# Expert weights in 4096-byte runs, shared rows written plainly, three experts in two passes, another order of experts

## The chip, the cores and the metric

The kernel runs on one core of a Trainium2 chip. The core has TensorE (PE) for matrix products with its own weight load (PEld), VectorE (DVE), ScalarE (ACT), GpSimd (POOL) and SyncE (SP), and 16 DMA engines that move data between HBM and the on-chip memory. Plain loads and stores are issued here by SP (queue q1 in the profile), gathers and scatter-adds by POOL (queue q0). The metric is the device time of one run in microseconds (us).

## The reference, cut to what matters

One decoder layer is computed for 1032 tokens (1024 of a prompt, 8 of decoding requests) of width 1024: a projection, two branches (RWKV-7 mixing and latent attention), a layer norm, and then a mixture of experts, which is what the change touches:

```python
def _swiglu(x, wg, wu, wd):
    return (jax.nn.silu(x @ wg) * (x @ wu)) @ wd

def _moe(h, P):
    ...
    _, e_idx = lax.top_k(jnp.where(e_mask, sb, -jnp.inf), TOP_K)        # 8 of 64 experts for a token
    ...
    routed = _routed_experts(h, e_idx, wts, P['w_exp_gate'], P['w_exp_up'], P['w_exp_down'])
    return routed + _swiglu(h, P['w_sh_gate'], P['w_sh_up'], P['w_sh_down'])
```

Each of the 64 experts has three fp32 matrices of 1024 x 256 elements (gate, up, down), 1 MB each, so 3 MB for an expert and 192 MB for all. Every token goes through 8 experts and through one shared expert of the same size. The results, weighted, are summed by token, and a last layer norm follows.

## The kernel before

The stages stand one behind the other: projections, the two branches, the output product with routing, the experts, the last norm. The experts take the last two fifths of the time.

**Ranks and capacities.** Experts are ranked on the chip by how many tokens chose them. For rank `r` the program is compiled for `CAPS[r]` rows: 480, 448, 416, 384, ... down to 68 for ranks 0 to 41, 64 for ranks 42 to 53, 32 for ranks 54 to 63. Only the expert's number is read at run time (`value_load` in `moe`, L2090), and it gives the address of the weights.

**Four ways to compute an expert.** From 200 rows up (`up_wide`) the gate and up weights are split in a high and a low part in fp32r (`part`: ACT writes `eph`, L1358, and DVE writes `epl`, L1361), the rows too, and three products are summed; the columns of a matrix product are the rows of the expert. From 65 to 128 rows (`up_rows`) the roles of weights and rows are exchanged. From 129 to 199 rows (`up_mid`) and up to 64 rows (`few`) the weights are used as they came, in plain fp32. The down product of all but `few` splits the down weights (`edh`, `edl`); what is left over at the end of an expert, up to 64 rows, goes through `down_rest` (L1967) with the plain weights.

**Loads.** SP issues them in the order of the program. `ffn_load` makes four tiles `egu` of 512 KB for an expert, each filled by two DMAs (gate and up, L1809), in which each partition reads 512 fp32 elements, a run of 2048 bytes; then two tiles `ewd` of 512 KB with the down weights (L1817), runs of 4096 bytes. There are 7 `egu` buffers (1.75 experts) and 6 `ewd` buffers (3 experts). A load waits until its buffer has been read by its last user, and whatever SP has behind it waits too. In `moe`, while expert `q` is computed, all of expert `q + 2` is issued.

**Rows.** For expert `q + 1` POOL gathers the rows of `h2D` with indirect DMAs of 128 KB (`xg`, L1841), DVE transposes them (L1844) into `xt` (two buffers, split into the one `xh`, `xl`) or, for `up_mid` and `few`, into `xf` (two buffers of 192 columns). Results are scaled by ACT and DVE into `ey` (four buffers of 1024 columns) and added to one of two accumulators in HBM, `accD`, by an indirect accumulating DMA from POOL (`add_rows`, L1981), taking turns.

**The shared expert** is computed first, in three passes of 360, 360 and 312 rows, with weights that are kept until the third pass has used them; its results are added to the accumulators like all others, by the index tile `IT`. Both accumulators are filled with zeros long before (20 DMAs of up to 512 KB, L1518).

**The order of the experts** is made by `order` (L2042): it takes large and row-exchanged experts in turn with middle and small ones, so that a running estimate of TensorE's lead over the loads stays near zero. By their rows the experts come as 128, 64, 120, 64, 112, 64, 112, 192, 108, 184, 480, 64, 104, 64, 448, 64, 100, 176, 96, 176, 416, 64, 92, 64, 384, ... and at the end 80, 136, 80, 32, 76, 32, 72, 32, 72, 32, 68, 32. The two later passes of the shared expert stand at places 0 and 1. Within this, a scheduler decides how the instructions of neighbouring experts are mixed on each engine.

## Time and profile before

| | us |
|---|---|
| median of 3 runs | 2481.7 (2474.22 to 2485.76) |
| the profiled execution | 2478.88 |
| its span, from the first to the last instruction | 2477.1 |
| start of routing's end and the shared expert | about 1385 |
| first routed expert computed from | about 1502 |
| last weights of an expert issued | 2377.9 |
| last norm's first loads of the sums | 2402.4 |

The page's own line on the span gives 86% for PE, 68% for PEld, 57% for DVE, 40% for ACT and 38% for POOL. These are averages over stages with different limits; the stage of the experts is read by itself, with windows. "DMA share" in such a window is the time that the packets took, divided by 16 engines times the window: it goes a little over 1 where packets overlap. The times of a window, a timeline row and a wait count from the start of the span.

### The profile page before, as it was taken

To read this page: it belongs to the slowest core of one execution; us is meant where nothing else is said; L and a number is where in the kernel's file an instruction comes from. 1 tells how busy PE (TensorE), PEld (TensorE's weight loads), DVE (VectorE), ACT (ScalarE), POOL (GpSimd) and SP (SyncE) were. 2 spreads that over 40 slices of the span, in tenths; PEclk is the share of its full clock that TensorE was granted. 3 is DMA by queue.
4 is the path that set the end of the run, shared out by engine and by line. 5 is a ranking of instruction groups with operands and counts; after the bars stand their busy time and mean duration, and the time that the engine had idled before them with its cause. 6 is when DMAs were issued, how large, how long until landed. Compare 5 with 4: busy or idle time off the path is not lost. (4 is left out here: it accounts for less than half of the span.)

```text
span 2477.1 us, 39847 instructions
## 1 busy us (share of the span) xinstructions
PE 2141.3 (86%) x14376; PEld 1695.0 (68%) x14376; DVE 1402.8 (57%) x2638; ACT 981.0 (40%) x1737; POOL 943.8 (38%) x799
## 2 busy tenths in 40 slices
PE   5999999978779998999689578899999998899754
PEld 3998999867557766578678466576767777677331
DVE  3544345511567865544657856566666666566437
ACT  3333332612445554222337434443443443344325
POOL 3243342021101001310216755467666566565226
PEclk8999999989789999999899699999999999899877
DMA  8146567454543424664999768999999999999994
GB/s 295 35 102 169 164 175 171 132 167 126 181 108 108 137 49 182 228 197 145 314 218 198 162 168 258 324 307 308 321 323 292 310 313 336 261 293 295 322 319 157
DMA packets 361507, 536.91 MB, mean 217 GB/s; under 512 B 118127, under 2 KB 219455, under 8 KB 354955
## 3 DMA queue, kind: packets, MB, share of 16 engines
q1 hardware_dynamic: 298330, 421.38, 53.3%
q0 software_dynamic: 60496, 112.63, 18.7%
q8 instruction: 114, 1.87, 0.3%
q10 hardware_dynamic: 2480, 0.33, 0.1%
q14 instruction: 87, 0.70, 0.1%
HBM read 410.97 MB, written 123.84 MB: 216 GB/s over the span
## 5 line engine op out<-in xcount | busy, mean ns | idle before, releaser
L1841 POOL DMA_INDIRECT xg<-h2D,IG x303 | 352.3, 1163 | 256.3 <-DVE xt L1844 92.2
L1361 DVE TENSOR_TENSOR epl<-egu,eph 128x1024 fp32r<-128x1024 f32 x140 | 169.5, 1217 | 114.6 <-ACT eph L1358 114.4
L147 PE MATMUL psup<-xh,eph 128*128 128x360 f32 (+15 forms) x576 | 184.8, 330 | 27.1 <-ACT xh L1358 19.2
L1358 ACT ACTIVATE eph<-egu 128x1024 fp32r<-128x1024 f32 x140 | 147.1, 1055 | 152.6 <-DMA egu<-in_w_exp_up_dram 87.7
L149 PE MATMUL psup<-xh,epl 128*128 128x360 f32 (+15 forms) x576 | 180.6, 326 | 10.7 <-DVE epl L1361 10.2
L148 PE MATMUL psup<-xl,eph 128*128 128x360 f32 (+15 forms) x576 | 186.0, 326 | 4.3 <-DVE xl L1361 4.2
L1981 POOL DMA_INDIRECT accD<-ey,IS x65 | 115.4, 1775 | 118.0 <-ACT ey L1974 57.6
L147 PE MATMUL psy<-edh,ehh 128*128 128x512 f32 (+12 forms) x296 | 127.1, 435 | 18.3 <-ACT ehh L1358 9.4
L1361 DVE TENSOR_TENSOR edl<-ewd,edh 128x1024 fp32r<-128x1024 f32 x90 | 108.5, 1217 | 54.6 <-ACT edh L1358 53.2
L147 PEld LDWEIGHTS psup<-xh,eph 128*128 128x128 f32 x576 | 113.3, 199 | 37.1 <-ACT xh L1358 21.3
L1358 ACT ACTIVATE edh<-ewd 128x1024 fp32r<-128x1024 f32 x90 | 94.0, 1053 | 89.2 <-PE psy L149 74.7
L147 PE MATMUL pwg<-hh,whg 128*128 128x344 f32 x384 | 126.7, 330 | 0.0
L149 PEld LDWEIGHTS psup<-xh,epl 128*128 128x128 f32 x576 | 111.6, 197 | 20.8 <-DVE epl L1361 11.9
L149 PE MATMUL pwg<-hh,wlg 128*128 128x344 f32 x384 | 125.2, 326 | 0.0
L148 PE MATMUL pwg<-hl,whg 128*128 128x344 f32 x384 | 125.0, 326 | 0.0
L148 PE MATMUL psy<-edl,ehh 128*128 128x512 f32 (+12 forms) x296 | 121.6, 416 | 0.0
L148 PEld LDWEIGHTS psup<-xl,eph 128*128 128x128 f32 x576 | 114.1, 198 | 10.4 <-DVE xl L1361 5.6
L1844 DVE STREAM_TRANSPOSE xt<-xg 128x1024 f32<-128x1024 f32 (+3 forms) x61 | 113.8, 1872 | 0.2
L149 PE MATMUL psy<-edh,ehl 128*128 128x512 f32 (+12 forms) x296 | 109.1, 412 | 0.6 <-DVE ehl L1361 0.5
L1994 PE MATMUL psup<-egu,xf 128*32 128x128 f32 (+1 forms) x1024 | 81.7, 335 | 23.9 <-DMA egu<-in_w_exp_up_dram 18.0
L1920 PE MATMUL psup<-xf,egu 128*128 128x176 f32 (+7 forms) x640 | 96.2, 304 | 1.9 <-DMA egu<-in_w_exp_gate_dram 1.8
L1920 PEld LDWEIGHTS psup<-xf,egu 128*128 128x128 f32 x640 | 92.1, 191 | 5.9 <-DMA egu<-in_w_exp_gate_dram 2.2
(723 smaller groups left out, 5747.8 us busy)
## 6 DMA issues: line engine op xcount, KB each, us to landing
egu<-in_w_exp_gate_dram SPq DMA_DIRECT2D x256, 256.0 KB
egu<-in_w_exp_up_dram SPq DMA_DIRECT2D x256, 256.0 KB
ewd<-in_w_exp_down_dram SPq DMA_DIRECT2D x128, 512.0 KB
wada<-in_w_ada_dram SPq DMA_DIRECT2D x24, 1024.0 KB
accD<-zero SPq DMA_DIRECT2D x18, 512.0 KB
gateD<-g SPq DMA_DIRECT2D x16, 516.0 KB
bg<-gateD SPq DMA_DIRECT2D x48, 172.0 KB
wrg<-in_w_in_dram SPq DMA_DIRECT2D x16, 512.0 KB
```

The lines of the kernel that those rows point to most:

```text
L147: nc.tensor.matmul(out, lh, rh, start=start, stop=False)
L148: nc.tensor.matmul(out, lh, rl, start=False, stop=False)
L149: nc.tensor.matmul(out, ll, rh, start=False, stop=stop)
L1358: nc.scalar.activation(hi, src, AF.Copy)
L1361: self.last_split = nc.vector.tensor_sub(lo, src, hi.bitcast(F32))
L1841: nc.gpsimd.indirect_dma_start(out=X[:, g, :], out_offset=None, in_=h4, in_offset=bass.IndirectOffsetOnAxis(ap=idx(j, g), axis=0))
L1844: nc.vector.transpose(out=dst.rearrange("p k (g b) -> p g k b", b=32), in_=X[:, 0:G, :].rearrange("p g (a k) -> p g k a", k=8))
L1920: nc.tensor.matmul(p[:, :C], gu[k // 2][:, j, k % 2, m * 128:(m + 1) * 128], xt[:, k, :C], start=(k == 0), stop=(k == 7))
L1981: self.nc.gpsimd.indirect_dma_start(out=acc, in_=y, in_offset=None, compute_op=OP.add, out_offset=bass.IndirectOffsetOnAxis(ap=idx, axis=0))
L1994: nc.tensor.matmul(ps[q * C:q * C + C, 0:2 * F].rearrange("p (a f) -> p a f", a=2), xt[:, k, :C], gu[k // 2][:, :, k % 2, q * F:q * F + F] ...
```

## The change

- Gate and up weights come in two tiles of 1 MB for an expert instead of four of 512 KB. Each DMA moves 512 KB in runs of 4096 bytes (`up_load`). There are 5 such buffers (2.5 experts) and 4 `ewd` buffers (2 experts).
- In `moe`, gate and up of expert `q + 2` are issued, and behind them the down weights of expert `q + 1` (`down_load`).
- The shared expert's results are written to `accD[0]` by plain DMAs from POOL, and only the 128 rows behind the tokens and all of `accD[1]` are filled with zeros. `IT` goes.
- Experts with over 384 rows (480, 448, 416) are computed in two passes, of 256 rows and of the rest (224, 192, 160), with the same weights; `xh`, `xl` and others have 384 columns instead of 480. The rests of 192 and 160 rows go through `up_mid`.
- `few` has its own row tiles `xs` (three of 64 columns); `xf` has one buffer instead of two. `down_rest` writes to `eys`, three tiles of 512 columns, instead of `ey`.
- The order is a list of numbers. By their rows the passes come as 64, 288, 64, 64, 112, 64, 256 and 160 (416), 344, 32, 216, 32, 120, 144, 336, 32, 104, 192, 96, ... and at the end 88, 176, 312, 64, 32, 100, 64, 256 and 224 (480), 32, 76, 32, 108, 32, 112.

```diff
-NU, XF, EP, ED, EY, XG, XT, EH, EWD = 7, 2, 3, 2, 4, 4, 2, 1, 6
-NB = dict(w=480, egu=NU, ewd=EWD, ed=ED, ep=EP, ey=EY, xt=XT, xg=XG)
+NU, XF, EP, ED, EY, XG, XT, EH, EWD = 5, 1, 3, 2, 4, 4, 2, 1, 4
+NB = dict(w=384, egu=NU, ewd=EWD, ed=ED, ep=EP, ey=EY, xt=XT, xg=XG)
...
+ORDER = [51, 9, 53, 52, 27, 48, 2, 5, 54, 13, 55, 26, 23, 6, 60, 30, 15, 32, 21, 3, 45, 25, 42, 10, 16, 36, 22, 37, 19, 8,
...
-        self.zeros = [(self.h2D, NT)] + [(a, r) for a in self.accD for r in range(0, NROW, 128)]
+        self.zeros = [(self.h2D, NT), (self.accD[0], NT)] + [(self.accD[1], r) for r in range(0, NROW, 128)]
...
-    def ffn_load(self, src, pool, between=None):
+    def up_load(self, src, pool):
 
         nc = self.nc
         gu = []
-        for kk in range(4):
-            t = pool.tile([128, 2, 2, 256], F32, tag='egu', name='egu', bufs=self.nb['egu'])
+        for half in range(2):
+            t = pool.tile([128, 2, 4, 256], F32, tag='egu', name='egu', bufs=self.nb['egu'])
             for j in range(2):
-                nc.sync.dma_start(t[:, j].rearrange("p k f -> p (k f)"),
-                                  src[j].rearrange("o (p k) f -> p (o k f)", p=128)[:, kk * 512:kk * 512 + 512])
-            gu.append(t)
-        if between:
-            between()
+                self.last_load = nc.sync.dma_start(t[:, j].rearrange("p k f -> p (k f)"),
+                                                   src[j].rearrange("o (p k) f -> p (o k f)", p=128)[:, half * 1024:half * 1024 + 1024])
+            gu += [t[:, :, 0:2], t[:, :, 2:4]]
+        return gu
+
+    def down_load(self, src, pool):
+
+        nc = self.nc
         wd = []
         for k in range(2):
             t = pool.tile([128, 1024], F32, tag='ewd', name='ewd', bufs=self.nb['ewd'])
             self.last_load = nc.sync.dma_start(t, src[2].rearrange("o (k p) f -> p (o k) f", p=128)[:, k])
             wd.append(t)
-        return gu, wd
+        return wd
...
     def x_plain(self, C, idx, pool):
-        xt = self.gpool.tile([128, 8, 192], F32, tag='xf', name='xf', bufs=XF)
+        if C <= 64:
+            xt = self.gpool.tile([128, 8, 64], F32, tag='xs', name='xs', bufs=3)
+        else:
+            xt = self.gpool.tile([128, 8, 192], F32, tag='xf', name='xf', bufs=XF)
...
-        y = pool.tile([128, 1024], F32, tag='ey', name='ey', bufs=self.nb['ey'])
+        y = pool.tile([128, 512], F32, tag='eys', name='eys', bufs=3)
...
-            if hf:
+            if hf and first is not None:
+                r0 = first + j * 128
+                nc.gpsimd.dma_start(self.accD[0][r0:r0 + n, :], y[:n])
+            elif hf:
                 self.add_rows(y[:n], ia(j, n), 1)
...
+        out = []
+        for r in ORDER:
+            c = CAPS[r]
+            out += [(r, 0, c)] if c <= self.nb['w'] else [(r, 0, 256), (r, 2, c - 256)]
         return out
...
-        load(0)
+        up(0)
+        down(0)
         rows(0)
-        load(1)
-        for q, r in enumerate(order):
+        up(1)
+        for q, (r, j0, C) in enumerate(order):
             if q + 2 < len(order):
-                load(q + 2)
+                up(q + 2)
             if q + 1 < len(order):
+                down(q + 1)
                 rows(q + 1)
```

How the change moves instructions is shown at three places. The first is SP in the middle of the experts: the loads of one expert before, and the first of the next. The numbers behind `egu` and `ewd` tell the tiles apart; between two loads stands a register instruction, left out here.

```order
L1809 DMA egu_16147<-in_w_exp_gate_dram 128x512
L1809 DMA egu_16147<-in_w_exp_up_dram 128x512
L1809 DMA egu_16150<-in_w_exp_gate_dram 128x512
L1809 DMA egu_16150<-in_w_exp_up_dram 128x512
L1809 DMA egu_16153<-in_w_exp_gate_dram 128x512
L1809 DMA egu_16153<-in_w_exp_up_dram 128x512
L1809 DMA egu_16156<-in_w_exp_gate_dram 128x512
L1809 DMA egu_16156<-in_w_exp_up_dram 128x512
L1817 DMA ewd_16159<-in_w_exp_down_dram 128x1024
L1817 DMA ewd_16161<-in_w_exp_down_dram 128x1024
L1809 DMA egu_16293<-in_w_exp_gate_dram 128x512
```

The same place of SP in the changed kernel:

```order
L1821 DMA ewd_16642<-in_w_exp_down_dram 128x1024
L1821 DMA ewd_16644<-in_w_exp_down_dram 128x1024
L1810 DMA egu_16699<-in_w_exp_gate_dram 128x1024
L1810 DMA egu_16699<-in_w_exp_up_dram 128x1024
L1810 DMA egu_16702<-in_w_exp_gate_dram 128x1024
L1810 DMA egu_16702<-in_w_exp_up_dram 128x1024
L1821 DMA ewd_16705<-in_w_exp_down_dram 128x1024
L1821 DMA ewd_16707<-in_w_exp_down_dram 128x1024
L1810 DMA egu_16801<-in_w_exp_gate_dram 128x1024
```

Ten loads for an expert have become six, and the two `ewd` rows behind a group of `egu` rows now belong to the expert before that group.

The second place is POOL at the shared expert, where the first gathers (`xg`) and the first results stand. Before:

```order
L1841 DMA xg<-h2D,IG 128x256 x12
L1981 DMA accD_5031<-ey,IT 1160x1024
L1981 DMA accD_5030<-ey,IT 1160x1024
L1841 DMA xg<-h2D,IG 128x256 x6
L1981 DMA accD_5031<-ey,IT 1160x1024
L1841 DMA xg<-h2D,IG 128x256 x4
```

And now:

```order
L1849 DMA xg<-h2D,IG 128x256 x11
L2036 DMA accD_5030<-ey 128x1024 x2
L1849 DMA xg<-h2D,IG 128x256 x2
L2036 DMA accD_5030<-ey 104x1024
L1849 DMA xg<-h2D,IG 128x256 x8
L2036 DMA accD_5030<-ey 128x1024 x2
```

The nine scatter-adds through `IT` are nine plain stores, at nearly the same places behind the gathers.

The third place is PE at the expert with 480 rows. Before, its up product begins between the down products of its neighbour:

```order
L1920 MATMUL psup<-xf,egu 128x184
L147 MATMUL psup<-xh,eph 128x480
L148 MATMUL psup<-xl,eph 128x480
L147 MATMUL psy<-edh,ehh 128x512 x2
L149 MATMUL psup<-xh,epl 128x480
```

Now, where its first pass ends and its second begins (`psup` is the up product, `psy` the down product):

```order
L149 MATMUL psup<-xh,eph 128x256
L150 MATMUL psup<-xl,eph 128x256
L151 MATMUL psup<-xh,epl 128x256
L149 MATMUL psup<-xh,eph 128x224 x4
L149 MATMUL psy<-edh,ehh 128x512
L150 MATMUL psy<-edl,ehh 128x512
```

The 96 products of 480 columns have become 96 of 256 and 96 of 224, and the down product of the first pass stands inside the up product of the second.

## Rows read from the trace of the kernel before

**Rows 1.** Windows: the end of routing with the shared expert, the routed experts, and the end. Columns: window and its length, then for PE, PEld, DVE, ACT and POOL the busy us and the instructions, the granted clock of TensorE, the DMA share and the rate in GB/s.

```profile
core 0: us, PE busy (x) PEld busy (x) DVE busy (x) ACT busy (x) POOL busy (x), PEclk, DMA share, GB/s
1410.00:1500.00 90.00, 75.51 (x386) 66.30 (x386) 52.26 (x86) 33.41 (x43) 49.38 (x43) 0.89 0.69 171
1500.00:2390.00 890.00, 795.31 (x4858) 592.44 (x4856) 556.25 (x618) 376.25 (x555) 509.01 (x383) 0.95 0.99 309
2390.00:2477.00 87.00, 30.99 (x104) 16.33 (x104) 53.36 (x67) 34.53 (x55) 46.12 (x23) 0.66 0.50 188
```

**Rows 2.** The DMA queues in the window from 1500 to 2390 us: packets, MB, share of the 16 engines' time.

```profile
DMA packets 118794, 275.15 MB, mean 309 GB/s; under 512 B 17117, under 2 KB 19293, under 8 KB 118716
...
q1 hardware_dynamic: 90313, 198.74, 63.8%
q0 software_dynamic: 28403, 75.46, 34.8%
```

**Rows 3.** The DMA view of four windows of 3 us in which only queue q1 moved data: 1752 to 1755 and 2345.5 to 2348.5 (gate and up weights alone, packets of 2 KB), then 2386 to 2389 and 2382 to 2385 (packets of 4 KB alone: the last down weights and the loads of `fx`).

```profile
DMA packets 626, 1.13 MB, mean 378 GB/s; under 512 B 72, under 2 KB 72, under 8 KB 626
q1 hardware_dynamic: 626, 1.13, 102.9%
...
DMA packets 442, 0.82 MB, mean 272 GB/s; under 512 B 49, under 2 KB 49, under 8 KB 441
...
DMA packets 347, 1.25 MB, mean 418 GB/s; under 512 B 41, under 2 KB 41, under 8 KB 347
q1 hardware_dynamic: 347, 1.25, 102.5%
...
DMA packets 295, 1.05 MB, mean 351 GB/s; under 512 B 39, under 2 KB 39, under 8 KB 294
```

**Rows 4.** The page's part on DMA issues: count and size of the weight loads and of the fills with zeros.

```profile
egu<-in_w_exp_gate_dram SPq DMA_DIRECT2D x256, 256.0 KB
egu<-in_w_exp_up_dram SPq DMA_DIRECT2D x256, 256.0 KB
ewd<-in_w_exp_down_dram SPq DMA_DIRECT2D x128, 512.0 KB
...
accD<-zero SPq DMA_DIRECT2D x18, 512.0 KB
```

**Rows 5.** Windows of 10 us within 1500 to 2390 us, columns as in rows 1. Of the 89 windows 14 have a DMA share under 0.95 and 63 one of 1.00 or more; shown are the first and the last of the 14 and the three lowest.

```profile
1530.00:1540.00 10.00, 10.00 (x38) 7.24 (x35) 6.67 (x7) 4.21 (x5) 5.58 (x4) 0.73 0.75 272
...
2100.00:2110.00 10.00, 7.33 (x42) 6.33 (x41) 0.00 (x0) 0.00 (x0) 7.87 (x8) 0.90 0.61 186
2110.00:2120.00 10.00, 5.68 (x31) 3.31 (x32) 3.87 (x5) 3.87 (x6) 4.92 (x4) 0.66 0.73 126
...
2220.00:2230.00 10.00, 7.73 (x30) 6.09 (x31) 7.55 (x9) 4.28 (x6) 2.45 (x3) 0.66 0.60 187
...
2340.00:2350.00 10.00, 7.57 (x62) 4.42 (x62) 1.65 (x4) 1.20 (x3) 0.65 (x1) 0.61 0.89 263
```

**Rows 6.** What SP's queue waited for between 1500 and 2390 us: us in total, times, longest.

```profile
SPq L1809 <- DMA ewd<-in_w_exp_down_dram: 118.4, 87, 3.4
SPq L1809 <- DMA egu<-in_w_exp_up_dram: 95.7, 81, 5.7
...
SPq L1817 <- PE psy L1967: 40.1, 7, 20.0
SPq L1809 <- DVE epl L1361: 40.0, 21, 5.5
SPq L1809 <- PE psup L1994: 33.9, 9, 13.9
```

**Rows 7.** Timeline of PE around 1690 us and around 2090 us: start us, duration us, instruction.

```profile
1689.64 0.36 PE L147 MATMUL psup<-xh,eph 128*128 128x448 f32 x1
1689.85 0.36 PE L148 MATMUL psup<-xl,eph 128*128 128x448 f32 x1
1690.05 0.36 PE L149 MATMUL psup<-xh,epl 128*128 128x448 f32 x1
...
2089.84 0.28 PE L148 MATMUL psup<-xl,eph 128*128 128x256 f32 x1
2089.96 0.28 PE L147 MATMUL psup<-xh,eph 128*128 128x256 f32 x1
2090.08 0.28 PE L148 MATMUL psup<-xl,eph 128*128 128x256 f32 x1
```

**Rows 8.** Groups between 1500 and 2390 us: the split of gate and up tiles, 512 KB each (busy us, mean ns, then idle time before).

```profile
L1361 DVE TENSOR_TENSOR epl<-egu,eph 128x1024 fp32r<-128x1024 f32 x126 | 152.5, 1216 | 98.7 <-ACT eph L1358 98.5
...
L1358 ACT ACTIVATE eph<-egu 128x1024 fp32r<-128x1024 f32 x125 | 131.3, 1055 | 120.0 <-DMA egu<-in_w_exp_up_dram 87.7 <-PE psup L148 16.5 <-PE psup L149 10.4
```

**Rows 9.** The view of tile `accD`: durations on the issuing engine (min, median, max ns), first and last start; then the time to landing. Last, from the DMA view of 1481.4 to 1485.4 us, in which only scatter-adds of the shared expert moved data.

```profile
L1518 SPq DMA_DIRECT2D accD<-zero x20: 460/1164/1671, 782.3 to 935.7; - x20
...
L1981 POOL DMA_INDIRECT accD<-ey,IT x9: 1583/1646/2280, 1457.9 to 1520.8; - x9
...
DMA to landing us min/median/max: 3.8/8.8/12.4
...
q0 software_dynamic: 212, 0.80, 106.5%
```

**Rows 10.** The window in which the zeros are written, columns as in rows 1.

```profile
780.00:940.00 160.00, 149.10 (x1646) 114.15 (x1647) 118.99 (x382) 86.41 (x210) 7.50 (x12) 0.97 0.43 131
```

**Rows 11.** The end of the experts, from the timelines of SP, PE and POOL: last loads of weights, last expert (32 rows), last scatter-add, first loads of the sums.

```profile
2377.11 0.33 SPq L1809 DMA_DIRECT2D egu<-in_w_exp_up_dram  x1
2377.94 0.96 SPq L1817 DMA_DIRECT2D ewd<-in_w_exp_down_dram  x2
...
2383.73 0.94 PE L1994 MATMUL psup<-egu,xf 128*32 128x128 f32 x26
2385.92 1.07 PE L1967 MATMUL psy<-ewd,ehs 128*32 128x256 f32 x16 [0.32 <-ACT ehs L2007]
...
2387.81 1.58 POOL L1981 DMA_INDIRECT accD<-ey,IG  x1 [1.34 <-ACTq L2125]
...
2402.43 1.75 SPq L2172 DMA_DIRECT2D fa<-accD  x4
```

More of the change, by code (lines that the diff above doesn't have):

```diff
@@ L66, in layout_constants @@
     parts['ph'] = (p // 64)[:, None]
-    parts['itok'] = np.tile(np.array([c + 128 * i for c, _ in SH for i in range(4)])[None, :], (128, 1))
     parts['rep64'] = (p[:, None] % 64 == j[None, :] % 64)
@@ L1482, in tail_setup @@
         nc.vector.tensor_copy(self.onebf, self.c('ones'))
-        self.IT = self.lp.tile([128, 3, 4], I32, name='IT')
-        nc.vector.tensor_scalar(self.IT, self.c('itok').rearrange("p (a j) -> p a j", a=3), self.c('pidx'), None, op0=OP.add)
         self.scat = []
@@ L2027, in many @@
             o = C - n
-            self.down_rest(r, o // 128, wd, [h[:, o:o + 128 // q] for h in hs], q, pool)
+            self.down_rest(r, j0 + o // 128, wd, [h[:, o:o + 128 // q] for h in hs], q, pool)
     def shared_rows(self, c0, C, pool):
@@ L2042, in order @@
     def order(self):
-        kinds = [[r for r in range(64) if f(CAPS[r])] for f in
-                 (lambda c: c >= 200, lambda c: 64 < c <= 128, lambda c: 128 < c < 200, lambda c: c <= 64)]
-        big, row, mid, few = kinds
-        lead, out = 25.0, []
-        def take(a, b, pe):
-            nonlocal lead
-            l = a if (lead < 0 and a) or not b else b
-            r = l.pop(0)
-            out.append(r)
-            lead += pe(CAPS[r]) - 8.8 - CAPS[r] * 0.024
-        wide = lambda c: 0.04 * c + 2.65 * -(-c // 128) + (0.4 if c >= 200 else 4 - 0.04 * c + 1.6)
-        narrow = lambda c: 5.7 if c <= 64 else 0.055 * c + 5.3
-        while big or row or mid or few:
-            if big or row:
-                take(big, row, wide)
-            if mid or few:
-                take(mid, few, narrow)
-        return out
-    def shared_load(self, pool, between=None):
-        return self.ffn_load([self.I[nm] for nm in ('w_sh_gate', 'w_sh_up', 'w_sh_down')], pool, between)
+        out = []
+        for r in ORDER:
+            c = CAPS[r]
+            out += [(r, 0, c)] if c <= self.nb['w'] else [(r, 0, 256), (r, 2, c - 256)]
+        return out
     def shared(self, a, w, x, pool, **kw):
-        self.many(SH[a][1], w, x, lambda j, n: self.IT[:n, a, j:j + 1], lambda j, n: 1.0, pool, **kw)
+        self.many(SH[a][1], w, x, None, lambda j, n: 1.0, pool, first=SH[a][0], **kw)
     def shared_first(self, pool):
         x = []
-        w = self.shw = self.shared_load(pool, lambda: x.append(self.shared_rows(*SH[0], pool)))
+        src = [self.I[nm] for nm in ('w_sh_gate', 'w_sh_up', 'w_sh_down')]
+        gu = self.up_load(src, pool)
+        x.append(self.shared_rows(*SH[0], pool))
+        w = self.shw = gu, self.down_load(src, pool)
         parts = [self.part(w[0][i], pool, 'ep', self.nb['ep']) for i in range(3)]
@@ L2080, in moe, with up, down @@
         nc = self.nc
[L2081 to L2088 removed]
+        order = [(-1 - a, 0, SH[1 + a][1]) for a in range(2)] + self.order()
+        loads, w, x, src = [self.last_load] * 3, {}, {}, {}
+        def up(q):
+            r, j0, C = order[q]
+            if r < 0:
+                w[q] = self.shw
+            elif j0:
+                w[q] = w[q - 1]
+            else:
                 with self.tc.issue_after(loads[q].ins):
[L2090 to L2093 removed]
+                    src[q] = self.expert_src(nc.sync.value_load(self.eid[0:1, r:r + 1], min_val=0, max_val=63))
+                w[q] = [self.up_load(src[q], pool), None]
             loads.append(self.last_load)
+        def down(q):
+            if q in src:
+                w[q][1] = self.down_load(src[q], pool)
         def rows(q):
[L2097 to L2100 removed]
+            r, j0, C = order[q]
+            x[q] = self.x_rows(C, lambda j, g: self.IG[:, j0 + j, g, r:r + 1], pool) if r >= 0 else self.shared_rows(*SH[-r], pool)
+        up(0)
+        down(0)
         rows(0)
[L2102 to L2103 removed]
+        up(1)
+        for q, (r, j0, C) in enumerate(order):
             if q + 2 < len(order):
[L2105 removed]
+                up(q + 2)
             if q + 1 < len(order):
+                down(q + 1)
                 rows(q + 1)
```

32 lines of the change are left out of this document (12 added, 20 removed).

## The prediction

> **What bounds the kernel now.** I read the windows of the stages first, then the DMA queues in the longest of them, then what SP waits for, and last whether any engine could be the bound instead. The windows show three parts of the last 1067 us: 90 us at the end of routing with a DMA share of 0.69, then 890 us of routed experts with a DMA share of 0.99, then the last norm at 0.50 [rows 1]. A reader should see that 0.99 as a mean over 890 us, at 309 GB/s, and compare it with windows of 10 us: in 63 of 89 the share is 1.00 or more, 1.04 in their mean, because packets overlap a little; in 14 it is under 0.95, with a mean of 0.78 [rows 5]. So the DMA engines are full for nearly all of the stage, and what they lack is 14 x 10 us x (1.04 - 0.78), some 36 us, in holes. The queue tells the same from the issuing side: SP's longest sums of waits are for DMAs that are still moving (118.4 us in 87 short waits, 95.7 in 81) [rows 6]; that is a queue that is full, not one that starves.
>
> Could an engine be the bound? PE is busy 795 of 890 us [rows 1], which looks like 89%. But products overlap: three products of 448 columns last 0.36 us each and start 0.20 us apart, those of 256 columns last 0.28 and start 0.12 apart [rows 7]. Counted by starts PE has a good deal of room; DVE (556 of 890 us), POOL (509) and ACT (376) have more. So I take the stage as bound by DMA time: what saves packet time saves wall time, and what adds work to an engine costs little while that room lasts.
>
> **The runs.** All gate and up loads, 512 of 256 KB or 134 MB [rows 4], change from packets of 2 KB to packets of 4 KB. Where queue q1 was alone and full, 2 KB packets moved 378 GB/s and 4 KB packets 418 in a good stretch, 272 and 351 in a bad one [rows 3]. 134 MB take 355 or 321 us by the good pair, a gain of 34 us, and 493 or 382 by the bad pair, a gain of 111. As a check by packets: 102.9% of 16 engines for 3 us over 554 packets of data is 89 ns for one of 2 KB, 102.5% over 306 is 161 ns for one of 4 KB, so two of the small cost 17 ns more than one of the large, 35 us over 32768 pairs. Over the stage q1 moved 198.74 MB in 63.8% of 890 us [rows 2], 350 GB/s, about a quarter of the way from the good to the bad figure, which would be -54 us; but those 350 hold stretches beside q0 too. I take -38 us, near the good pair, with 0 and -111 as ends.
>
> Against this stands a rule of the Trainium skill ("DMA: Bandwidth & Descriptors", section "Specifications"): a transfer reaches line rate from 512 bytes on. By that rule 2048 bytes are as good as 4096 and this term is 0; the trace, with 378 against 418 GB/s, does not agree, though the two kinds of packets were seen at different places and from different tensors.
>
> **Buffers and order.** The 36 us of holes come when SP stands at a buffer that is still in use: 40.1 us in 7 waits for a down product (L1817, longest 20.0), 40.0 us for the split of a gate/up tile, 33.9 us for a product of a small expert [rows 6]. Gate and up now have 2.5 experts of buffers instead of 1.75, so SP can run ahead by three quarters of an expert more; `ewd` falls from 6 to 4, but its loads come later, behind the next expert's gate and up, so that the same older expert must be done with its down weights at the same point of the stream. Large experts no longer stand together in the middle, with weights alone to move at the end. This could take all the holes away (-36 us), or double them, if the listed order suits the chip worse (+36). I take -12 us, a third, since the coarser tiles come free later.
>
> **Start of the experts.** The nine results of the shared expert, 1032 rows of 4 KB, go out as plain stores. A scatter-add packet cost 106.5% of 16 engines for 4 us over 196 packets of data, 348 ns [rows 9]; a plain store is not in the trace, and I bound it by that and by the 161 ns of a plain load: 0 to 12 us of DMA time, in a stretch where the share is 0.69 and most of it is hidden. Before the third shared pass lets go of the weights, 3 MB of routed gate and up can be loaded instead of 1.5 MB, 4 us at 378 GB/s. I take -5 us for both, ends 0 and -16. On POOL nine indirect adds of 1.65 us [rows 9] become direct stores, which only helps. The fills with zeros lose 9 of 512 KB, 4.7 MB at 780 to 940 us, where the DMA share is 0.43 and PE is busy 149 of 160 us [rows 9, 10]: 0, and no more than the 11 us in which PE was idle. The slightly changed mixing of instructions before the experts: 0, ends -5 and +5.
>
> **Two passes.** The expert of 480 rows splits its four gate/up tiles and two down tiles twice, those of 448 and 416 their two down tiles (their rests use plain weights for the up product): ten more splits, 10.6 us on ACT and 12.2 on DVE by 1055 and 1216 ns each [rows 8]. The cover is the DMA bound: DVE goes from 556 to 568 of 890 us. On PE, 96 products of 480 columns, 0.22 us apart if 448 columns take 0.20, become 96 at 0.12 and 96 at about 0.11 [rows 7], 1 us more. No new bytes are loaded. Where DVE or PE happens to be late at that place up to 14 us show; I take +2. The rests of 192 and 160 rows take fewer products than before and I put them at 0, ends -5 and +5.
>
> **The end.** The last expert now has 32 rows: from its first product at 2383.7 to its scatter-add at 2387.8 pass 4.1 us, and the sums are loaded from 2402.4 [rows 11]. With 112 rows the last half of the gate/up weights still needs two splits one behind the other (1.06 + 2 x 1.22 = 3.5 us), 12 products of 512 columns at about 0.23 (2.8), activation, split and transpose (about 1.5), and 12 down products (2.8): about 10.6 us, so +6, ends 0 and +10.
>
> **The sum.** -38 - 12 - 5 + 2 + 6 = -47 us against the profiled execution's 2478.9, that is 2432. The median of the runs shown lies 2.8 us above the profiled one, so I predict 2435 us.
>
> **Rivals.**
> 1. The runs bring nothing, because the two rates of rows 3 differ by tensor and place and not by packet, and the holes stay. For it: 2 KB packets too reached 378 GB/s, near the 4 KB ones in their bad stretch (351). Against it: packets of either size cost about a fixed part more than their bytes, 89 against 161 ns. Then -5 + 2 + 6 = +3, or 2485 us. This is the rule of 512 bytes from the Trainium skill, named above.
> 2. More than forecast: the runs give -54 by the stage's own rate and the holes close to a few us (-30 instead of -12): 2435 - 16 - 18 = 2401 us. For it: the deeper gate/up buffers, and loads in flight that are twice as large, so that a short stop of SP empties nothing. Against it: the same scatter-adds and gathers still take 34.8% of the engines' time [rows 2].
> 3. Slower: SP stops at `ewd`. With 4 buffers the down load of expert q + 1 needs the down product of q - 1 finished, the leftover product of `down_rest` included, and everything behind it on SP stands: the gate and up weights of q + 3. Before, this wait came 7 times at 5.7 us in the mean, with 6 buffers [rows 6]. If a third of the experts meet it, 14 times more, that is +80 us: 2515. The point from which it decides is about 8 more such waits, 47 us. Against it: the loads ahead of it are larger now and keep the engines fed longer.
> 4. An engine becomes the bound: PE by its 89%, as the busy share reads. Then the runs give nothing and the added splits and passes show, 2485 + 14 = 2499 us. The starts of rows 7 speak against it.
>
> **How the numbers follow.** Forecast 0.60, with its own range from 2412 to 2465; rival 1 0.13; rival 2 0.16; rival 3 0.08; rival 4 0.03. The measurement can tell about 0.5%, so faster means under 2469 us and slower over 2494. Faster: 0.58 of the forecast and all of rival 2 and a little of rival 1, 0.76. Same: 0.14. Slower: rivals 3 and 4 with the tail of the others, 0.10. The range takes in the middle of rival 2 and rival 1's price: 2397 to 2487.
>
> **What would show it.** In the changed profile, q1's packets in the stage of the experts should fall by about 32000 at the same bytes, and full stretches of gate/up loads should move about 400 GB/s or more; if they stay near 378 and 272, the runs were wrong. The stage from the first routed expert to the last weights should be 40 to 50 us shorter, at a DMA share that stays near 1; a lower share with the old length would mean that an engine or a buffer took over, and SP's waits would name it: `ewd` for a down product (rival 3), or `egu` for a split. The end, from the last weights issued to the first loads of the sums, should grow from 24 us to about 30. The prediction is wrong as a whole if the bytes per us in the stage of the experts do not rise above 309 GB/s.

## The result and the profile after

| | before | after |
|---|---|---|
| median, us | 2477.96 (2472.57 to 2485.76) | 2444.28 (2441.13 to 2452.79) |
| ratio, 95% interval | | 0.9875 [0.9851, 0.9899] |
| profiled execution, span | 2478.88, 2477.1 | 2443.09, 2441.3 |
| first load of a routed expert | 1410.4 | 1413.2 |
| last load of weights | 2378.6 | 2336.3 |
| first load of the sums | 2402.4 | 2366.6 |

The kernel is 1.25% faster, 34 us by the medians and 36 us in the profiled executions. Those 36 us divide as the table shows: the experts begin 2.8 us later, their loads take 45.1 us less (968.2 before, 923.1 now), and the stretch behind the last weights grew by 6.5 us (23.8 before, 30.3 now).

The windows of the changed kernel, in the columns of [rows 1]; its experts end some 40 us earlier, so the second window is 40 us shorter:

```profile
1410.00:1500.00 90.00, 79.30 (x422) 68.96 (x423) 58.49 (x98) 35.32 (x46) 43.48 (x44) 0.91 0.63 195
1500.00:2350.00 850.00, 770.72 (x5039) 590.82 (x5037) 555.80 (x625) 377.37 (x565) 519.40 (x382) 0.96 0.97 319
2350.00:2441.00 91.00, 38.38 (x118) 19.93 (x118) 54.55 (x73) 38.03 (x61) 49.54 (x25) 0.64 0.55 195
```

The bytes per us rose from 309 to 319 GB/s while the DMA share fell from 0.99 to 0.97, and PE is now busy 771 of 850 us. So the packets became cheaper, but not all of what they saved became time. Two views say how much cheaper they became. First the queues from 1500 to 2340 us, as in [rows 2]:

```profile
DMA packets 80938, 267.79 MB, mean 319 GB/s; under 512 B 12907, under 2 KB 14955, under 8 KB 80868
...
q1 hardware_dynamic: 52808, 192.29, 60.8%
q0 software_dynamic: 28060, 74.60, 36.0%
```

Queue q1 moved 192.29 MB in 60.8% of 840 us, 376 GB/s while in use; the same measure of the kernel before, from 1500 to 2380 us, is 194.94 MB in 63.4% of 880 us, 349 GB/s. Over the 201 MB of all experts that is 576 us against 535. Second, a window of 3 us (1744 to 1747) in which, but for one packet of instructions (q8), only gate and up weights moved, as in [rows 3]:

```profile
DMA packets 341, 1.25 MB, mean 418 GB/s; under 512 B 38, under 2 KB 38, under 8 KB 340
...
q1 hardware_dynamic: 340, 1.24, 103.1%
```

The same tensors that reached 378 GB/s in packets of 2 KB reach 412 in packets of 4 KB, by the 1.24 MB of q1 alone. Counted packet by packet over the stage, a packet of 2 KB on q1 took 84 ns in the median and 96 in the mean before, one of 4 KB takes 159 and 173 now: two of the small cost 20 ns more than one of the large.

What SP's queue waited for from 1500 to 2350 us, as in [rows 6]:

```profile
SPq L1821 <- PE psy L1978: 193.9, 39, 18.1
SPq L1810 <- DMA egu<-in_w_exp_up_dram: 62.7, 27, 6.6
SPq L1821 <- DVE edl L1363: 61.7, 17, 10.0
SPq L1810 <- DVE epl L1363: 55.7, 13, 9.9
```

Before, the waits for moving DMAs led (118.4 and 95.7 us). Now SP stands at a tile of down weights (L1821) that a down product still reads: 39 times instead of 7, 193.9 us instead of 40.1. The holes, stretches in which the DMA engines lack work, grew with it: of 84 windows of 10 us from 1500 to 2340, 19 have a DMA share under 0.95 (14 of 89 before, [rows 5]), 0.78 in their mean, so 19 x 10 x (1.04 - 0.78), some 50 us, are missing, not 36. The two emptiest:

```profile
2220.00:2230.00 10.00, 7.84 (x34) 5.33 (x33) 4.48 (x5) 4.83 (x5) 7.49 (x6) 1.00 0.50 107
1580.00:1590.00 10.00, 10.00 (x65) 9.34 (x64) 9.50 (x10) 6.04 (x10) 4.21 (x3) 1.00 0.51 160
```

In the second PE has no idle moment; the first lies just ahead of a place that comes back below. The end, from SP's and POOL's timelines, as in [rows 11]:

```profile
2333.53 3.09 SPq L1821 DMA_DIRECT2D ewd<-in_w_exp_down_dram  x4
2359.50 1.48 POOL L1992 DMA_INDIRECT accD<-ey,IS  x1 [6.48 <-ACTq L2132]
2366.61 3.80 SPq L2179 DMA_DIRECT2D fa<-accD  x8
```

And the plain stores of the shared rows, in the columns of [rows 9]; they were indirect adds of 1646 ns:

```profile
L2036 POOL DMA_DIRECT2D accD<-ey x9: 565/605/652, 1455.5 to 1518.4; - x9
```

### The profile page after: what moved, and what is told of

It is laid out like the page before. It is cut to its first block, busy times and chain, and to the rows that moved or that the text cites. A ratio compares the mean times of both kernels' runs of the same rounds, so it can differ in the third digit from the quotient of the medians.

```text
span 2441.3 us, 39301 instructions
## 1 busy us (share of the span) xinstructions
PE 2129.5 (87%) x14600; PEld 1700.3 (70%) x14600; DVE 1409.2 (58%) x2655; ACT 987.3 (40%) x1755; POOL 949.1 (39%) x799
## 5 line engine op out<-in xcount | busy, mean ns | idle before, releaser
L149 PE MATMUL psup<-xh,eph 128*128 128x256 f32 (+13 forms) x608 | 181.8, 307 | 7.6 <-ACT eph L1360 4.9
L150 PE MATMUL psup<-xl,eph 128*128 128x256 f32 (+13 forms) x608 | 182.4, 303 | 1.3 <-DVE eh L1895 1.3
L151 PE MATMUL psup<-xh,epl 128*128 128x256 f32 (+13 forms) x608 | 176.4, 303 | 0.1
L1992 POOL DMA_INDIRECT accD<-ey,IS x65 | 118.9, 1829 | 118.2 <-ACT ey L1985 40.1
L1363 DVE TENSOR_TENSOR edl<-ewd,edh 128x1024 fp32r<-128x1024 f32 x96 | 116.5, 1220 | 53.6 <-ACT edh L1360 53.3
L149 PE MATMUL psy<-edh,ehh 128*128 128x512 f32 (+14 forms) x296 | 123.4, 431 | 27.3 <-ACT ehh L1360 17.0
L150 PE MATMUL psy<-edl,ehh 128*128 128x512 f32 (+14 forms) x296 | 122.1, 416 | 1.1 <-DVE edl L1363 1.0
L1931 PE MATMUL psup<-xf,egu 128*128 128x160 f32 (+7 forms) x768 | 117.3, 306 | 3.1 <-DVE eh L1880 3.1
L1931 PEld LDWEIGHTS psup<-xf,egu 128*128 128x128 f32 x768 | 112.1, 191 | 9.8 <-DVE eh L1880 4.0
L151 PE MATMUL psy<-edh,ehl 128*128 128x512 f32 (+14 forms) x296 | 113.1, 413 | 3.6 <-DVE ehl L1363 3.6
L1671 POOL DMA_INDIRECT tabD<-pairs,dest x72 | 77.8, 1081 | 40.4 <-issue 18.9
```

Of the source, the lines that this page charges most:

```text
L149: nc.tensor.matmul(out, lh, rh, start=start, stop=False)
L150: nc.tensor.matmul(out, lh, rl, start=False, stop=False)
L151: nc.tensor.matmul(out, ll, rh, start=False, stop=stop)
L1363: self.last_split = nc.vector.tensor_sub(lo, src, hi.bitcast(F32))
L1671: i = nc.gpsimd.indirect_dma_start(out=self.tabD, in_=pr[:n, j, :], in_offset=None, out_offset=bass.IndirectOffsetOnAxis(ap=di[:n, j:j + 1 ...
L1931: nc.tensor.matmul(p[:, :C], gu[k // 2][:, j, k % 2, m * 128:(m + 1) * 128], xt[:, k, :C], start=(k == 0), stop=(k == 7))
```

## The experiments

Theory: the longer runs are the gain, about 40 us; the rest of the change gives back some, as PE became a limit of nearly the same length as the transfers. Rivals: the gain comes from buffers, order and plain stores; or something third holds both. The runs were made in sets on several chips (the kernel before took 2474 to 2522 us, median by set), so they are compared by their ratio to before, and one of them is the changed kernel again. 1% is about 25 us.

| run | what | ratio, 95% interval |
|---|---|---|
| e13_after_again | the change once more | 0.9869 [0.9837, 0.9900] |
| e1_runs2k | the change without the long runs | 1.0049 [1.0016, 1.0083] |
| e9b_before4k_ewd5 | long runs alone | 0.9939 [0.9911, 0.9967] |
| e10_pe_relief | a third of the split products left out | 0.9821 [0.9767, 0.9875] |
| e11_dma_relief | 32.5 MB of down weights not loaded | 0.9827 [0.9772, 0.9881] |
| e12_both | both | 0.9646 [0.9611, 0.9680] |
| e8_down | down weights behind their own gate/up | 1.0112 [1.0072, 1.0152] |
| e3_order | the order of before | 0.9938 [0.9914, 0.9962] |
| e5_tail | last expert 32 rows | 0.9948 [0.9926, 0.9969] |
| e6_shadd | shared rows by scatter-add | 0.9872 [0.9843, 0.9900] |
| e2c_ewd5_xs1 | 5 buffers `ewd`, 1 `xs` | 1.0034 [1.0011, 1.0056] |
| e14_xs1 | 1 buffer `xs` | 0.9819 [0.9765, 0.9873] |

**e1_runs2k: the same kernel with runs of 2048 bytes**

```diff
-            for j in range(2):
-                self.last_load = nc.sync.dma_start(t[:, j].rearrange("p k f -> p (k f)"),
-                                                   src[j].rearrange("o (p k) f -> p (o k f)", p=128)[:, half * 1024:half * 1024 + 1024])
+            for kk in range(2 * half, 2 * half + 2):
+                for j in range(2):
+                    o = kk % 2 * 2
+                    self.last_load = nc.sync.dma_start(t[:, j, o:o + 2].rearrange("p k f -> p (k f)"),
+                                                       src[j].rearrange("o (p k) f -> p (o k f)", p=128)[:, kk * 512:kk * 512 + 512])
```

Expected: 

> The kernel after, but each 1 MB tile of gate and up weights is filled by four transfers of 256 KB in runs of 2048 bytes (as before) instead of two of 512 KB in runs of 4096; tiles, buffers, orders and all else are those of after (2444 us). Theory (the runs are the gain: the queue of the weights moved 349 GB/s while in use before and 376 after, 42 us over the 201 MB of the experts): 2480 to 2490 us, as slow as before, and the queue's rate falls back to about 350. Rival 1 (the runs bring nothing, the gain came from buffers, order and the plain stores): 2440 to 2450. Third way (the stage of after is already held by TensorE, which waited only 7 us for weights): slower by less than the queue's own loss, 2455 to 2475.

Measured 2518.57 us, 0.5% slower than before where the change is 1.3% faster: the runs are worth 1.8%, some 45 us, beside the other edits. The queue q1 of this kernel, from 1500 to 2410 us:

```profile
q1 hardware_dynamic: 89225, 193.43, 60.9%
```

That is 193.43 MB in 554 us, 349 GB/s, the rate of before to the digit. The changed kernel on another chip (e13_after_again), from 1500 to 2360 us:

```profile
q1 hardware_dynamic: 52968, 192.90, 59.6%
```

Here 192.90 MB take 513 us, 376 GB/s again. The runs are the gain, and all other edits together cost 12 us without them (4 to 21 by the interval). Rival 1 falls. The edit also doubles the number of transfers, each of which ends in a few small packets; but over the stage these took only 7 us of the 16 engines' time here and 4 in e13, while two packets of 2 KB took 192 ns in the mean against 173 for one of 4 KB. So it is the length of the packets, and not the number of transfers, that made nearly all of the difference in q1's time. The rule of the Trainium skill ("DMA: Bandwidth & Descriptors", section "Specifications") that transfers reach line rate from 512 bytes on, cited in the prediction, does not hold in this kernel: 349 against 376 GB/s.

**e9b_before4k_ewd5: the long runs alone, in the kernel before**

```diff
-NU, XF, EP, ED, EY, XG, XT, EH, EWD = 7, 2, 3, 2, 4, 4, 2, 1, 6
+NU, XF, EP, ED, EY, XG, XT, EH, EWD = 4, 2, 3, 2, 4, 4, 2, 1, 5
-        for kk in range(4):
-            t = pool.tile([128, 2, 2, 256], F32, tag='egu', name='egu', bufs=self.nb['egu'])
+        for half in range(2):
+            t = pool.tile([128, 2, 4, 256], F32, tag='egu', name='egu', bufs=self.nb['egu'])
...
```

Expected: 

> The kernel before with one part of the change alone: gate and up weights in tiles of 1 MB by 4096-byte runs (4 tiles, and 5 buffers of down weights instead of 6, for the room). Order of experts, scatter-adds of the shared rows, one pass of the largest and down weights behind their own gate and up stay as before. Theory (the runs are the gain, about 40 us, and the rest of the change gives little or costs some): 2435 to 2450 us. Rival (the runs gain only with the new order of loads, because four 1 MB tiles in the old order leave two experts at most in flight): 2455 to 2480. Rival 1 (runs bring nothing): 2475 to 2485 or more.

Measured 2491.95 us, 0.9939 of before or 15 us faster, as the rival had it: a third of what the runs give in e1. Queue q1 from 1500 to 2385 us:

```profile
q1 hardware_dynamic: 52860, 192.51, 58.1%
```

SP's waits there:

```profile
SPq L1817 <- PE psy L1967: 134.5, 19, 33.3
SPq L1809 <- PE psup L1994: 70.8, 15, 10.5
```

The packets are as cheap as in the change (192.51 MB in 514 us, 374 GB/s), but SP stands for engines 134.5 us at down weights (40.1 before) and 70.8 at gate and up (33.9). Runs alone give 15 us, the rest alone costs 12, both give 32: either part is worth more with the other. Which of the other edits the large tiles need is not parted here, as this run also has other numbers of buffers (4 and 5 against 5 and 4); e8 and e3 below show that the place of the down loads and the order of the experts both weigh.

**e13_after_again, e10_pe_relief, e11_dma_relief, e12_both: which limit holds**

e13_after_again is the changed kernel. The relief of TensorE (e10, e12) computes two of the three split products; the relief of the transfers (e11, e12) gives every second expert the down weights of the expert before it, the last line pair here:

```diff
+    def mm2(self, out, l, r, start, stop):
+        nc = self.nc
+        nc.tensor.matmul(out, l[0], r[0], start=start, stop=False)
+        nc.tensor.matmul(out, l[0], r[1], start=False, stop=stop)
...
-                    self.mm3(ps[:n, :], (hh[:, k, s], hl[:, k, s]), (w[k][0][:, c], w[k][1][:, c]), k == 0, k == 1)
+                    self.mm2(ps[:n, :], (hh[:, k, s], hl[:, k, s]), (w[k][0][:, c], w[k][1][:, c]), k == 0, k == 1)
...
-                w[q][1] = self.down_load(src[q], pool)
+                w[q][1] = w[q - 1][1] if q % 2 and order[q - 1][0] >= 0 else self.down_load(src[q], pool)
```

Expected of the change again: 

> The kernel after, unchanged, beside the others of this set on one chip: the ratio to before was 0.9875 [0.9851, 0.9899] when it was first timed; 0.985 to 0.990 is expected again. It is what the other three are to be set against, and it tells whether the ratio holds on another chip, where the kernel before takes another time.

Expected of the relief of TensorE: 

> The kernel after without the last of the three products of each split matmul of the experts and shared rows (low part of the one operand by high part of the other), so a third of those matmuls is left out, some 180 us of the 771 us that TensorE was busy in 1500:2350; every transfer, split and wait stays. If the holes of the weights' transfers (50 us below 1.04 in 84 windows) come from buffers that TensorE releases late (TensorE is what holds the stage since the runs got longer): faster by 25 to 50 us, 2395 to 2420, and the 10-us windows under 0.95 of DMA become few. If the holes come from the queue's own order (SP standing at a tile of down weights while gate and up buffers are free) or from gathers and adds: faster by less than 12 us.

Expected of the relief of the transfers: 

> The kernel after without the down weights of 31 of the 64 experts (each of these uses those of the expert before it): 32.5 MB fewer are moved, 86 us of the queue at the 376 GB/s it had in the experts; all computation stays. If the transfers are still what sets the stage: faster by 60 to 86 us, 2358 to 2384. If TensorE holds it (771 us busy and 76 us of waits for its own splits and copies in 850): faster by under 20 us, 2424 or more. Between these, both take turns.

Expected of both: 

> The kernel after with both reliefs at once: a third of the split matmuls of the experts left out, and the down weights of 31 experts not loaded (they use those of the expert before). Alone, the ratios to before were 0.982 and 0.983, some 12 us below that of after each. If TensorE and the transfers are two limits of nearly the same length, so that either relief alone runs into the other: far more than the sum of the two, 50 us or more below after, ratio 0.967 or less. If a third thing holds both (the splits on ScalarE and VectorE, the gathers and scatter-adds, SP's queue): about the sum, 15 to 30 us below after, ratio 0.976 to 0.982.

The window from the first load of a routed expert to the last weights, in the columns of [rows 1]; first the changed kernel (e13_after_again):

```profile
1434.00:2361.00 927.00, 841.53 (x5398) 655.99 (x5397) 605.27 (x709) 404.12 (x601) 547.87 (x415) 0.96 0.93 305
```

Without a third of the split products (e10_pe_relief):

```profile
1432.00:2365.00 933.00, 719.30 (x4380) 527.01 (x4379) 601.00 (x711) 403.47 (x601) 563.93 (x419) 0.86 0.93 303
```

Without 32.5 MB of transfers (e11_dma_relief):

```profile
1425.00:2361.00 936.00, 853.71 (x5392) 657.26 (x5391) 603.23 (x707) 402.97 (x599) 558.28 (x419) 0.96 0.88 269
```

Without either (e12_both):

```profile
1434.00:2296.00 862.00, 700.28 (x4373) 523.12 (x4371) 597.95 (x708) 399.63 (x599) 571.85 (x410) 0.89 0.91 290
```

Relief of PE brought 12 us by the ratios (2463.41 us), relief of the transfers 11 us (2464.77), both 56 us (2419.89), more than twice their sum. By the intervals each single relief brought anything from nothing to some 25 us, and in the traces neither makes the window shorter (933 and 936 us against 927); both together make it 65 us shorter (862). That is the sign of two limits of nearly the same length. With 32.5 MB less PE is busy 854 of 936 us and its waits for others sum to 66 us, so it sets the pace. With 122 us less of PE the transfers go on at 303 GB/s.

Of my two readings for e10 the first, that the holes come from buffers which PE releases late, fell: they did not close (of 84 windows from 1520 to 2360, 24 are under 0.95, and 20 in e13), and the gain was about 12 us, not 25 to 50. The freed PE waits at `psy` for ACT's copy of results, and ACT for landings of scatter-adds, in e10 and then in e13:

```profile
ACT ey L1990 <- DMA accD<-ey,IS: 64.8, 13, 12.7
```

```profile
ACT ey L1985 <- DMA accD<-ey,IS: 27.6, 6, 10.7
```

What makes these last holes isn't settled.

**e8_down: the down weights behind their own gate and up**

```diff
                 w[q] = [self.up_load(src[q], pool), None]
+                w[q][1] = self.down_load(src[q], pool)
...
-            if q in src:
-                w[q][1] = self.down_load(src[q], pool)
+            pass
```

Expected: 

> The kernel after, but the down weights of an expert are loaded right behind its own gate and up weights (as before), with the four buffers of down weights of after. Theory (rival 3 the other way round: SP stood 190 us at a tile of down weights in after, and with four buffers the old place makes it stand an expert earlier, with gate and up loads queued behind): slower than after by 5 to 25 us, ratio 0.990 to 0.998. Rival (the place is worth nothing, since the same bytes pass the same queue): within 4 us of after.

Measured 2541.3 us, 1.0112 of before: 60 us slower than the change, in the direction of the theory, but over twice its largest price. With four buffers, the place of the down load decides. The window of the experts:

```profile
1436.00:2441.00 1005.00, 871.70 (x5367) 665.86 (x5370) 607.20 (x710) 408.40 (x600) 530.66 (x415) 0.92 0.88 282
```

SP's waits in it:

```profile
SPq L1821 <- PE psy L1978: 209.0, 33, 34.7
SPq L1821 <- DVE edl L1363: 100.3, 20, 15.3
```

And the first of these waits in e13:

```profile
SPq L1821 <- PE psy L1978: 155.4, 29, 22.4
```

That sum is a third longer in e8, and the DMA share falls from 0.93 to 0.88. Yet all of SP's waits for anything but DMAs sum to 500 us in e8 and 471 in e13, so the sum does not tell the time. The length of a single stop does better. In e13 the stops of 4 to 8 us between two loads of weights come to 144 us, and queue q1 moved next to nothing in 16 of them; the stops of 16 us and more come to 76 us, and q1 stood empty in 52. In e8 these long stops come to 240 us, 154 of them empty. Summed over the window in steps of half a us, the time by which the DMA share stays under 1 grew from 88 to 149 us, most of the 78 us by which the window is longer. So here a stop costs little while loads are in flight, and nearly its length behind that.

**e3_order: the experts in the order of before**

```diff
-        out = []
-        for r in ORDER:
+        kinds = [[r for r in range(64) if f(CAPS[r])] for f in
+                 (lambda c: c >= 200, lambda c: 64 < c <= 128, lambda c: 128 < c < 200, lambda c: c <= 64)]
...
+        seq, out = out, []
+        for r in seq:
             c = CAPS[r]
             out += [(r, 0, c)] if c <= self.nb['w'] else [(r, 0, 256), (r, 2, c - 256)]
```

Expected: 

> The kernel after with the experts in the order that the planner of before gives (the three largest still in two passes, side by side). Theory (with the longer runs TensorE and the transfers are about even, and what is lost is lost where many small experts or many large ones follow each other; the new order spreads them better): slower than after by 5 to 20 us, ratio 0.990 to 0.996. Rival (the order was part of why the holes grew from 36 to 50 us): faster by 3 to 12 us, ratio 0.983 to 0.986. It also ends with an expert of 32 rows as before, which alone gives back about 6 us behind the last weights.

Measured 2497.41 us, 0.9938: 17 us slower than the change, as the theory had it, although it ends with 32 rows. The new order pays about two thirds of a per cent.

**e5_tail: the last expert has 32 rows again**

```diff
-         38, 59, 29, 56, 28]
+         38, 28, 59, 29, 56]
```

Expected: 

> The kernel after with its last four experts in another order: 84 or so rows of experts stay the same, but the expert of 112 rows is moved three places forward and the last one has 32 rows again. Theory (behind the last weights stand the splits, products and scatter-add of one expert of 112 rows: 30.3 us from the last load of weights to the first load of the sums, against 23.8 in before, of which 6.5 us is that expert): 4 to 8 us faster than after, ratio to before 0.984 (after: 0.987). Rival (the work only moves in front of the last weights, as TensorE is a limit too): within 3 us of after.

Both readings missed: 2463.17 us, 0.9948, 19 us slower than the change. The stretch behind the last weights did shrink, from 105 to 100 us up to the end of the span, but the weights ended 26 us later (974 us from the first load of the shared weights to the last weights, 948 in the change). SP's instructions stand in the same order in both, but on the other engines the scheduler mixed the last experts anew, on POOL from a place some 100 us before the swapped ones. POOL there, in the changed kernel:

```profile
2228.91 1.78 POOL L1992 DMA_INDIRECT accD<-ey,IS  x1 [1.30 <-ACT ey L1985]
2231.00 2.03 POOL L1992 DMA_INDIRECT accD<-eys,IC  x1 [0.30 <-issue]
2233.34 1.02 POOL L1849 DMA_INDIRECT xg<-h2D,IG  x1 [0.30 <-issue]
2234.66 0.97 POOL L1849 DMA_INDIRECT xg<-h2D,IG  x1 [0.31 <-issue]
...
2239.59 0.69 ACT L1985 ACTIVATE ey<-psy,L 128x512 f32<-128x512 f32 x1 [10.84 <-DMA accD<-ey,IS]
```

And in e5_tail, whose times run 1.6 us later here:

```profile
2228.48 1.01 POOL L1849 DMA_INDIRECT xg<-h2D,IG  x1 [0.30 <-issue]
2229.80 0.98 POOL L1849 DMA_INDIRECT xg<-h2D,IG  x1 [0.30 <-DMA accD<-ey,IS]
2231.09 1.27 POOL L1849 DMA_INDIRECT xg<-h2D,IG  x1 [0.30 <-issue]
2232.66 0.95 POOL L1849 DMA_INDIRECT xg<-h2D,IG  x1 [0.30 <-issue]
2233.91 1.82 POOL L1992 DMA_INDIRECT accD<-ey,IS  x1 [0.30 <-issue]
...
2246.59 0.69 ACT L1985 ACTIVATE ey<-psy,L 128x512 f32<-128x512 f32 x1 [16.33 <-DMA accD<-ey,IS]
```

Four gathers now stand ahead of the scatter-add that frees the next `ey` buffer. It starts 5.0 us later instead of 1.6, ACT and DVE stop at `ey` 16.3 and 15.0 us instead of 10.8 and 8.0, and all that is queued behind them, splits of weights too, is by then 7.0 us behind the changed kernel. The place lies just behind the emptiest window above. This explains at most 7 of the 26 us. The loads of weights fall back by some 8 us more at a stop of SP for a split (17.0 us instead of 9.9), and by 13 at the last two down tiles; why these two steps came is not shown.

**e6_shadd: shared rows by scatter-add, both sums zeroed**

```diff
-        self.many(SH[a][1], w, x, None, lambda j, n: 1.0, pool, first=SH[a][0], **kw)
+        self.many(SH[a][1], w, x, lambda j, n: self.IT[:n, a, j:j + 1], lambda j, n: 1.0, pool, **kw)
```

Expected: 

> The kernel after with the shared rows added by scatter-add into both sums, and both sums zeroed beforehand, as in before (nine scatter-adds for nine plain stores, and nine more stores of zeros). Theory (the start of the experts gained about 5 us: 2.3 MB more weights came in 1410 to 1500): 3 to 8 us slower than after, ratio about 0.989. Rival (the stage is held by TensorE and the transfers together over 900 us, and nine stores at its head don't show): within 3 us of after.

Measured 2441.06 us, 0.9872: nothing, within 0.3%. The rival holds. The early bytes did depend on the stores: from 1410 to 1500 us this kernel moved 182 GB/s, the change 195.

**e2c_ewd5_xs1 and e14_xs1: a fifth buffer of down weights, and the room it takes**

```diff
-NU, XF, EP, ED, EY, XG, XT, EH, EWD = 5, 1, 3, 2, 4, 4, 2, 1, 4
+NU, XF, EP, ED, EY, XG, XT, EH, EWD = 5, 1, 3, 2, 4, 4, 2, 1, 5
...
-            xt = self.gpool.tile([128, 8, 64], F32, tag='xs', name='xs', bufs=3)
+            xt = self.gpool.tile([128, 8, 64], F32, tag='xs', name='xs', bufs=1)
```

The first line is in e2c alone, the second in both.

Expected of e2c: 

> The kernel after with five buffers of down weights instead of four (and one buffer instead of three for the gathered rows of small experts, for the room). Theory (rival 3 of the prediction, small: SP stands 194 us in 39 waits at a tile of down weights, with gate and up loads behind it; holes of 50 us in the stage come from there): SP's waits for that tile fall by half or more, and the time by 5 to 20 us, ratio 0.979 to 0.985. Rival (SP's waits lie beside loads in flight, and TensorE is the other limit at 12 us below): within 4 us of after, or slower by a few us, as the rows of small experts are gathered later.

Expected of e14: 

> The kernel after with one buffer instead of three for the gathered rows of small experts, and the four buffers of down weights of after. It parts the two edits of the run before, which was 1.0034 of before where after is 0.987. Theory (the own tiles of small experts are a part of the change that pays: with one tile POOL stands at its gathers and the adds queue behind them; the fifth buffer of down weights brings next to nothing): ratio 0.998 to 1.010. Rival (the fifth buffer is what cost, as loads of weights run further ahead of the rows): ratio 0.985 to 0.991.

Measured 2481.3 us (1.0034) with both edits, 2473.58 us (0.9819, not to be told from the change) with the single `xs` alone. So the rival of e14 holds: the own tiles of small experts show no gain from being three, and the kernel with the fifth `ewd` buffer is some 2% slower than the one without (1.4 to 2.9 by the intervals), the opposite of what I expected of it. Nor did SP's waits at a tile of down weights fall, as I had expected. From e2c:

```profile
SPq L1821 <- PE psy L1978: 204.8, 27, 21.1
```

ACT's waits for landings over the experts, in e2c and then in e14:

```profile
ACT ey L1985 <- DMA accD<-ey,IS: 43.3, 5, 16.8
```

```profile
ACT ey L1985 <- DMA accD<-ey,IS: 19.8, 6, 6.5
```

The stops at `ey` are longer with the fifth buffer, as in e5_tail. The buffer also changes how the scheduler mixes the engines (some 2000 of PE's 14600 products stand at another place than in e14), and I could not give it without that; which of the two costs stays open. No variant that could be told from the change was faster than it and still computed everything.

## Why the prediction was right, and where it was not

The forecast was 2435 us and faster; measured were 2444.28. Against the profiled execution the sum said -47 us, and it gave -36. The sum takes its terms as independent of each other, and they are not: the runs are worth 45 us beside the other edits (e1) and 15 us in the kernel before (e9b), so the rest costs 12 us without the runs and gives some 17 with them. That the sum came so near is in part luck.

- **The runs, -38: right beside the other edits.** q1's time fell by 42 us, and undoing the runs alone costs 45 (e1). Alone in the kernel before they bring 15, although q1's packets are as cheap there (e9b). The sign and the rate of full stretches (412 GB/s) came as listed, and q1's packets fell by 36000 at nearly the same bytes, some 32000 of data and 4000 that close transfers.
- **Buffers and order, -12: wrong in its mechanism.** The step that failed is "I take -12 us, a third": the holes that were to shrink grew from 36 to 50 us. Either part alone opens more of them: by the same count e1 has some 67 us (22 of 91 windows from 1500 to 2410, 0.74 in their mean) and e9b some 65 (19 of 88 from 1500 to 2380, 0.69). All edits but the runs cost 12 us with short runs (e1) where I had -12 - 5 + 2 + 6 = -9; with the long runs they bring some 17. Behind it stands the step on PE, "Counted by starts PE has a good deal of room": e11 shows PE as a second limit, about 11 us behind the transfers. That PE's pace makes the holes is not shown, as e10 kept them with PE relieved. The -12 was also a net of large parts: the new order gives some 17 us (e3), and the new place of the down weights is worth 60 (e8) where `ewd` has four buffers.
- **Start, -5: 0** (e6). 195 instead of 171 GB/s came in early, as forecast, but it did not shorten the kernel. That the two limits behind it keep it from being used is argued, not shown.
- **Two passes, +2: not tried alone.**
- **The end, +6: 6.5.** Right as a stretch, but not to be had back: moved forward, the expert costs 19 us elsewhere (e5).
- **Rival 1** fell with e1, **rival 2** with the holes, which grew. **Rival 3** named the wait that came, but its price was wrong: I took each wait at its own length and let it decide from 47 us on, and it grew by 154 us in a kernel that became faster. A short stop costs little, because q1 still moves what is in flight (128 of 144 us in e13); a long one costs most of its length, as in e8. **Rival 4** was half right: PE is a limit, but it lies below the transfers, so the runs still gave most of their gain.

## What to carry to other kernels

When the bound resource gets faster, ask how long the next one is: a relief is worth no more than the distance to it, here some 12 us beyond the change, and only a run that relieves both shows that (56 us). Take an edit out of the changed kernel and also put it alone into the old one: where the two prices differ, as 45 and 15 us do here, they can't be added up. Price the waits of an issuing queue by how long the single stops last against what is in flight, not by their sum. Where a scheduler mixes the engines, a small edit is never alone; compare the order of instructions before blaming the edit.

## What the runs showed of the hardware that I had not expected

- The gain of 4096-byte over 2048-byte runs, 412 against 378 GB/s in full stretches and 376 against 349 over the whole stage, is shown in the rates and in the time of a packet; the second pair came again to the digit on other chips (349 with 2048-byte runs in e1, 376 with 4096 in e13), on which the kernel before takes 28 and 34 us longer as a whole.
- With a third of the split products left out, TensorE's granted clock over the experts fell from 0.96 to 0.86 in the mean (1 is the level of 2.4 GHz, 0.5 that of 1.2) and the 128x512 down products lasted 470 ns instead of 423 in their mean: TensorE waited for others 195 us there instead of 77. With the longer products it gave back part of its relief.
- A plain store of 512 KB kept POOL 605 ns, an indirect add 1646 ns, and over the whole kernel the difference of nine did not show.
